# Feed-forward norm in token layout with whole-bank copies, and six row buffers for the first expert blocks

## The chip, the cores and the metric

The kernel runs on one core of one Trainium2 chip. A core has TensorE (PE; its weight loads are listed as PEld), VectorE (DVE), ScalarE (ACT), GpSimd (POOL) and SyncE (SP), which issues most of the transfers between HBM and the on-chip memory SBUF. PE writes its results to PSUM, eight banks of 128 partitions by 512 fp32 words, and DVE and ACT read them there. Each engine works through its own queue in order. The metric is the device time of one execution in microseconds (us); lower is better.

## The reference, cut to what matters

One decoder layer over 512 tokens of 1024 features. Two mixers (a gated recurrence and sparse attention) are projected back and added to the residual stream; then comes an RMS norm with the gain `ffn_norm`, and a mixer of 16384 experts (128 x 128 product keys) that is fed by the normed tokens:

```python
h = h + mixed @ w_out[i]
h = h + peer_ffn(rmsnorm(h, ffn_norm[i]), peer_wq[i], peer_keys[i], peer_u[i], peer_v[i])

def rmsnorm(x, g):
    y = x * rsqrt(mean(x * x, axis=-1, keepdims=True) + EPS)
    return y * g
# peer_ffn, for a block of tokens xt:
q = xt @ wq                                    # 16 groups of 128 columns
s = einsum('thcd,hckd->thck', q, sub_keys)     # scores, then top-16, then experts and weights w
act = gelu(einsum('thkd,td->thk', u[expert], xt))
out = einsum('thk,thkd->td', w * act, v[expert])
```

## The kernel before

The program is written once in Python; a scheduler with priorities sets the order of the instructions on each engine, and memory pools set which buffer a transfer has to wait for. Precise products are made of three passes (`mm3`) over a high and a low half of each operand, and `split` makes the halves: ACT copies the source into the high half, DVE subtracts that from the source into the low half.

The parts that matter here, in order of time:

- **Attention and output projection** (to about 349 us). `out_tile(hf, tt)` transposes one 128-token tile of a mixer's output (4 PE transposes), splits it (`moh`, `mol`), multiplies it by the output weights (24 matmuls for two halves of 512 columns), adds it to the residual `h1` (DVE, L540) and sums squares (ACT, `junk`, L543). The last tile, token tile 0 of the attention half, is left for after the attention: `POST` says ("n",3), ("o",0), ("n",2), ("n",1), ("n",0), where "o" is that `out_tile` and "n" is `ffn_norm`.
- **The feed-forward norm** (`ffn_norm`, once per token tile). POOL makes the reciprocal root `rx`; DVE scales an identity with it (`dg`, L550); eight 128x128 matmuls with `dg` transpose and scale `h1` into two banks (L555); then eight times ACT copies 128 columns, scaled by the gain, into the high half `xTh` (L560; the trace calls the tile aTh), and DVE makes the low half `xTl` (L561; aTl).
- **Query projection and scores** (about 372 to 484 us): 16 rounds `hc`, each with a load of `wq` (tile `wr`), its split, 24 matmuls over `xTh`, `xTl`, and scores with the keys. The keys come in four loads `kr_`, whose halves `kyh`, `kyl` are made in rounds 0, 4, 8 and 12 of the program, that is, where the scheduler puts them.
- **Full blocks** (about 484 to 637 us). The expert table `uT` has 128 blocks of 512 KB. The first 20 are multiplied in full fp32 from the row buffer `ur` directly (L834, 8 matmuls each over `xf`, which the trace shows as two records per matmul), between the matmuls that spread the routing weights (L1036, L1037) into `wd`. `ur` has two buffers. Later blocks are split into `uh`, `ul` first.
- **Main loop** (about 700 to 1640 us): the other blocks, the `v` table, and gathered rows for token tile 0.

Of the kernel before, what the change touches and what calls it, by code (L numbers as in the profile page):

```python
# [10 lines left out]
F32 = mybir.dt.float32  # L11
# [6 lines left out]
ALU = mybir.AluOpType  # L18
# [51 lines left out]
HPLAN = [("h", 0), ("h", 1), ("kv", 0), ("h", 2), ("h", 3)]  # L70
KPLAN = [("q", 0), ("k", 0), ("k", 1), ("s", 0), ("s", 1), ("s", 2), ("s", 3), ("c", 0)]
PLAN = [("b",0),("b",1),("c",),("a",3,(1,2,0),4),("p",),("a",3,(1,2,0),8),("a",3,(1,2,0),ALL),("l",0),("o",0,2),("o",0,0),("o",0,1),("a",2,(1,2,0),5),("a",2,(1,2,0),ALL),("o",0,3),("l",1),("a",1,(1,0,2),ALL),("o",1,3),("o",1,2),("a",0,(1,0,2),3),("a",0,(1,0,2),ALL),("o",1,1)]
POST = [("n",3),("o",0),("n",2),("n",1),("n",0)]
APRI = 150
XB = 6
NP = 3
# [83 lines left out]
def _body(ctx, tc, a, out, dbg=None):  # L160
# [33 lines left out]
    def flat(ap):  # L194
        return ap.rearrange("p a b -> p (a b)")
# [319 lines left out]
            w.append((wh, wl))  # L515
        return w

    def out_tile(pool, pp, tag, bufs, w, hf, tt):
        src = (hv, nq)[hf]
        o = pp.tile([128, 512], F32, name=tag, bufs=bufs)  # L520
        for k in range(4):
            PE.transpose(o[:, k * 128:(k + 1) * 128], src[:, tt, k * 128:(k + 1) * 128], ident)
        mh = pool.tile([128, 4, 128], F32R, name="moh", bufs=MB)
        ml = pool.tile([128, 4, 128], F32R, name="mol", bufs=MB)
        split(flat(mh), flat(ml), o)
        outer = not hf and tt == LAST0
        os_ = [pp.tile([128, 512], F32, name=tag, bufs=bufs) for _ in range(2)] if outer else []
        for k in range(4 if outer else 0):
            for n in range(2):
                ns = slice(n * 512, (n + 1) * 512)  # L530
                mm3(os_[n], mh[:, k], ml[:, k], w[k][0][:, ns], w[k][1][:, ns], k == 0, k == 3)
        for n in range(2):
            ns = slice(n * 512, (n + 1) * 512)
            if outer:
                o = os_[n]
            else:
                o = pp.tile([128, 512], F32, name=tag, bufs=bufs)
                for k in range(4):
                    mm3(o, mh[:, k], ml[:, k], w[k][0][:, ns], w[k][1][:, ns], k == 0, k == 3)
            V.tensor_tensor(h1[:, tt, ns], h1[:, tt, ns], o, op=ALU.add)  # L540
            if hf:
                junk = pool.tile([128, 512], F32, name="junk")
                act(junk, h1[:, tt, ns], AF.Square, accum_out=ss[:, tt, n:n + 1])  # L543

    def ffn_norm(pool, pp, tag, bufs, tt):
        ts = slice(tt * 128, (tt + 1) * 128)
        G.tensor_tensor(rx[:, tt:tt + 1], ss[:, tt, 0:1], ss[:, tt, 1:2], op=ALU.add)
        rstd(rx[:, tt:tt + 1], rx[:, tt:tt + 1], 1, 1.0 / D)
        dg = pool.tile([128, 128], F32, name="dg", bufs=DGB)
        V.tensor_scalar(dg, ident, rx[:, tt:tt + 1], None, op0=ALU.mult)  # L550
        for q in range(2):
            o = pp.tile([128, 512], F32, name=tag, bufs=bufs)
            for k in range(4):
                c = 4 * q + k
                PE.matmul(o[:, k * 128:(k + 1) * 128], lhsT=h1[:, tt, c * 128:(c + 1) * 128], rhs=dg, start=True, stop=True)  # L555
            for k in range(4):
                c = 4 * q + k
                gc = gn[:, G_FFN + c:G_FFN + c + 1]
                ok = o[:, k * 128:(k + 1) * 128]
                act(xTh[:, c, ts], ok, AF.Copy, scale=gc)  # L560
                V.scalar_tensor_tensor(xTl[:, c, ts], ok, gc, xTh[:, c, ts].bitcast(F32), op0=ALU.mult, op1=ALU.subtract)  # L561

    dram = ctx.enter_context(tc.tile_pool(name="dram", bufs=1, space=DRAM))
    ppd = dram.tile([T, D], F32, name="ppd")
# [1 line left out]
    with ExitStack() as e2:  # L566
# [181 lines left out]
        for step in PLAN:  # L748
            if step[0] == "a":
                tt, order, n = step[1:]  # L750
                g = gens.setdefault(tt, attend(tt, order))
                tc.cur_priority -= APRI
                for _ in range(n):
                    next(g, None)
                tc.cur_priority += APRI
            elif step[0] == "b":
                blocks(step[1])
            elif step[0] == "c":
                compress()
            elif step[0] == "p":  # L760
                ple(wop)
            elif step[0] == "l":
                wo_ = out_load(wop, step[1])
            elif step[0] == "n":
                ffn_norm(wop, nps, "tp", NB_TP, step[1])
            else:
                out_tile(wop, nps, "tp", NB_TP, wo_, step[1], step[2])
# [23 lines left out]
    wp = wpx.enter_context(tc.tile_pool(name="wp", bufs=2, reuse_waits="tile"))  # L791
    with ExitStack() as e2:
        ps = e2.enter_context(tc.tile_pool(name="ps2", bufs=6, space=PSUM, reuse_waits="tile"))
        for name, tt in POST:
            if name == "n":
                ffn_norm(wop, ps, "mm", 6, tt)
            else:
                out_tile(wop, ps, "mm", 6, wo_, 1, tt)
        put("h1", h1)
        wox.close()  # L800
        den = ExitStack()
        dense = den.enter_context(tc.tile_pool(name="dense", bufs=2, side="right", reuse_waits="tile"))
        pre = ExitStack()
        prep = pre.enter_context(tc.tile_pool(name="prep", bufs=AHEAD, side="right", reuse_waits="tile"))
# [14 lines left out]
    def a_steps(full):  # L819
        b = nextb[0]  # L820
        nextb[0] += 1
        dq = nc.gpsimd if NPRE - HOLD <= b < NPRE else nc.sync
        ur = dense.tile([128, NC, 128], F32, name="ur")
        dq.dma_start(out=ur, in_=a["uT"][b])
        g_ = prep.tile([128, TD], F32, name="gp") if b < AHEAD else dense.tile([128, TD], F32, name="ga", bufs=3)
        ahead.append(g_ if b < AHEAD or b >= NPRE else None)
# [91 lines left out]
    with ExitStack() as e2:  # L918
# [4 lines left out]
        with ExitStack() as e3:  # L923
# [3 lines left out]
            for hc in range(17):  # L927
# [3 lines left out]
                if hc < 16:  # L931
                    raw = wp.tile([128, NC, 128], F32, name="wr")
                    nc.sync.dma_start(out=raw, in_=a["wq"][:, hc])
                    wh = wp.tile([128, NC, 128], F32R, name="wh")
                    if hc == 0:
                        kyh = wp.tile([128, 16, 128], F32R, name="kyh", bufs=1)
                        kyl = wp.tile([128, 16, 128], F32R, name="kyl", bufs=1)
                    wl = wp.tile([128, NC, 128], F32R, name="wl")
                    split(flat(wh), flat(wl), flat(raw))
                    if hc % 4 == 0:  # L940
                        kr_ = wp.tile([128, 4, 128], F32, name="kr_")
                        nc.sync.dma_start(out=kr_, in_=a["keys"][:, hc:hc + 4])
                        split(kyh[:, hc:hc + 4], kyl[:, hc:hc + 4], kr_)
                    o = ps.tile([128, 512], F32, name="mm")
                    for c in range(NC):
                        mm3(o, wh[:, c], wl[:, c], xTh[:, c], xTl[:, c], c == 0, c == NC - 1)
                    qh = wp.tile([128, T], F32R, name="qh")
                    ql = wp.tile([128, T], F32R, name="ql")
                    split(qh, ql, o)
                    qs.append((qh, ql))  # L950
# [338 lines left out]
```

## Time and profile before

| | us |
|---|---|
| median of 3 runs | 1702.3 (1701.36 to 1702.61) |
| profiled execution, its own time | 1700.27 |
| span of that execution in the trace | 1698.5 |
| mean granted clock of TensorE | 0.993 |

The runs are executions of the same program without a profiler. The profiled execution took 1700.27 us, 1.8 us more than the span from the first to the last instruction. All rows further down are from it, with times counted from the start of the span.

### The profile page before, as it was taken

The numbers are of one execution on the slowest core, as the hardware profiler recorded it, in microseconds if no ns is written. First come the engines' busy times: TensorE is split into PE (matmuls) and PEld (weight loads), VectorE is DVE, ScalarE is ACT, GpSimd is POOL, SyncE is SP. The second block draws the span as 40 slices with busy tenths as digits, with TensorE's granted clock in tenths as the row PEclk, the third lists the DMA queues.
The fourth block names the chain that finished last, engine by engine and source line by source line (L and its number), as shares of the span: only waits on it lengthen the run. The fifth ranks groups of instructions, "written<-read, shape, count | busy, mean of one in ns | idle before, by whom it ended". The sixth has DMA issues, their size and how long they took to land.

```text
span 1698.5 us, 24123 instructions
## 1 busy us (share of the span) xinstructions
PE 1650.0 (97%) x8864; PEld 1416.2 (83%) x8864; DVE 1260.3 (74%) x2485; ACT 745.3 (44%) x1291; POOL 486.1 (29%) x356
## 2 busy tenths in 40 slices
PE   9999999979999999999999999999999999999998
PEld 7887888768866668878899999999999999888987
DVE  6565745659999987865487877777878877787864
ACT  7443664652237875533333333333333333433342
POOL 0013000020000000000055655655545544455610
PEclk9999999989999999999999999999999999999999
DMA  7311130032214689967589898898898988899941
GB/s 256 112 50 49 45 100 25 26 101 86 63 50 146 203 259 287 309 222 239 171 302 327 309 337 313 323 331 325 318 324 323 322 318 322 319 329 333 328 140 50
DMA packets 148647, 373.38 MB, mean 220 GB/s; under 512 B 11990, under 2 KB 59734, under 8 KB 148526
## 3 DMA queue, kind: packets, MB, share of 16 engines
q1 hardware_dynamic: 109808, 231.46, 40.4%
q0 software_dynamic: 38720, 140.38, 23.3%
q8 instruction: 69, 1.13, 0.3%
q14 instruction: 50, 0.41, 0.1%
HBM read 339.02 MB, written 32.77 MB: 219 GB/s over the span
## 4 chain that ended last, share of the span: by engine, by line
PE 50%; issue 17%; DMA 15%; POOL 9%; DVE 5%; ACT 3%; SPq 0%; POOLq 0%; DVEq 0%; ACTq 0%
POOL row L1093 8%; DMA row<-v,eid 7%; PE ac L188 5%; PE ac L186 5%; PE ac L187 5%; PE mm L186 4%; PE mm L187 4%; PE mm L188 4%; PE apsum L834 3%; DMA ur<-uT 3%; DMA row<-u,eid 3%; PE apsum L188 3%; PE apsum L186 3%; PE apsum L187 3%; PE ob L708 2%
## 5 line engine op out<-in xcount | busy, mean ns | idle before, releaser
L188 PE MATMUL ac<-vh,pl 128*128 128x512 f32 x768 | 301.9, 394 | 1.9 <-DVE pl L192 1.7
L1093 POOL DMA_INDIRECT row<-u,eid x128 | 216.2, 1689 | 304.3 <-DVE hn L1097 246.3
L187 PE MATMUL ac<-vl,ph 128*128 128x512 f32 x768 | 301.1, 392 | 0.5 <-DVE vl L192 0.5
L186 PE MATMUL ac<-vh,ph 128*128 128x512 f32 x768 | 299.4, 391 | 1.9 <-ACT vh L191 1.0
L188 PE MATMUL apsum<-aTh,ul 128*128 128x384 f32 x864 | 290.4, 336 | 3.9 <-DVE ul L192 3.9
L186 PE MATMUL apsum<-aTh,uh 128*128 128x384 f32 x864 | 291.5, 337 | 0.5 <-ACT uh L191 0.5
L187 PE MATMUL apsum<-aTl,uh 128*128 128x384 f32 x864 | 289.6, 335 | 0.0
L1093 POOL DMA_INDIRECT row<-v,eid x128 | 208.8, 1631 | 184.0 <-DVE hn L1105 160.4
L191 ACT ACTIVATE uh<-ur 128x1024 fp32r<-128x1024 f32 x108 | 114.5, 1060 | 248.5 <-PE apsum L187 230.1
L192 DVE TENSOR_TENSOR ul<-ur,uh 128x1024 fp32r<-128x1024 f32 x108 | 132.1, 1223 | 78.5 <-ACT uh L191 78.3
L1105 DVE SCALAR_TENSOR_TENSOR hn<-row,cw__7013,hn 128x1024 f32<-128x1024 f32 x128 | 158.6, 1281 | 21.9 <-DMA row<-v,eid 21.7
L188 PEld LDWEIGHTS ac<-vh,pl 128*128 128x128 f32 x768 | 144.1, 188 | 34.8 <-DVE pl L192 4.8
L191 ACT ACTIVATE ph<-ga 128x384 fp32r<-128x384 f32 x118 | 62.0, 525 | 249.3 <-DVE ga L1154 194.6
L186 PEld LDWEIGHTS ac<-vh,ph 128*128 128x128 f32 x768 | 144.4, 188 | 30.7 <-ACT ph L191 2.2
L187 PEld LDWEIGHTS ac<-vl,ph 128*128 128x128 f32 x768 | 144.3, 188 | 29.2 <-DVE vl L192 1.2
L192 DVE TENSOR_TENSOR vl<-vr,vh 128x1024 fp32r<-128x1024 f32 x128 | 156.0, 1219 | 16.0 <-ACT vh L191 16.0
L188 PEld LDWEIGHTS apsum<-aTh,ul 128*128 128x128 f32 x864 | 162.8, 188 | 5.2 <-DVE ul L192 5.2
L191 ACT ACTIVATE vh<-vr 128x1024 fp32r<-128x1024 f32 x128 | 135.2, 1056 | 71.3 <-PE ac L188 70.4
L186 PEld LDWEIGHTS apsum<-aTh,uh 128*128 128x128 f32 x864 | 162.8, 188 | 4.5 <-ACT uh L191 0.6
L187 PEld LDWEIGHTS apsum<-aTl,uh 128*128 128x128 f32 x864 | 162.8, 188 | 3.9
L1097 DVE SCALAR_TENSOR_TENSOR hn<-row,hn 128x1024 f32<-128x1024 f32 x128 | 156.2, 1221 | 3.3 <-DMA row<-u,eid 1.8
L834 PE MATMUL apsum<-xf,ur 128*128 128x384 f32 x320 | 114.7, 503 | 9.5 <-DMA ur<-uT 9.5
(403 smaller groups left out, 2902.7 us busy)
## 6 DMA issues: line engine op xcount, KB each, us to landing
vr<-v SPq DMA_DIRECT2D x128, 512.0 KB, 5.4
ur<-uT SPq DMA_DIRECT2D x125, 512.0 KB, 6.4
xf<-wd SPq DMA_DIRECT2D x30, 768.0 KB, 8.3
wraw<-wi SPq DMA_DIRECT2D x20, 512.0 KB, 4.8
wd<-hn SPq DMA_DIRECT2D x5, 1664.0 KB, 8.7
wd<-stage SPq DMA_DIRECT2D x5, 1664.0 KB, 9.3
wr<-wq SPq DMA_DIRECT2D x16, 512.0 KB, 3.6
wor<-wo SPq DMA_DIRECT2D x16, 256.0 KB, 2.7
```

The source lines that it names most:

```text
L186: PE.matmul(o, lhsT=lh, rhs=rh, start=first, stop=False)
L187: PE.matmul(o, lhsT=lh, rhs=rl, start=False, stop=False)
L188: return PE.matmul(o, lhsT=ll, rhs=rh, start=False, stop=last)
L191: act(hi, src, AF.Copy)
L192: return V.tensor_tensor(lo, src, hi.bitcast(F32), op=ALU.subtract)
L708: PE.matmul(o_ps[:, h], lhsT=pt[:, k * 128:(k + 1) * 128], rhs=kv[:, k, 256 + i * 64:256 + (i + 1) * 64], start=(k == 0), stop=(k == tt))
L834: PE.matmul(o[:, :TD], lhsT=ur[:, c], rhs=xf[:, c], start=c == 0, stop=c == NC - 1)
L1093: G.indirect_dma_start(out=gt, out_offset=None, in_=table, in_offset=bass.IndirectOffsetOnAxis(ap=eid[:, slot:slot + 1], axis=0))
L1097: V.scalar_tensor_tensor(junk, gt, 1.0, xn0, op0=ALU.mult, op1=ALU.mult, accum_out=dots[:, s_:s_ + 1])
L1105: V.scalar_tensor_tensor(ak, gt, cw_[:, s_:s_ + 1], ak, op0=ALU.mult, op1=ALU.add)
```

## The change

Five edits. (1) `ffn_norm` multiplies `h1` by `rx` and by the gain in token layout (DVE, new L562, 512 columns at a time, into `xn`), transposes it plainly with the constant identity, and makes the halves of a whole bank with one `split`, so one ACT copy and one DVE subtraction per bank of four 128x128 blocks. (2) The gain comes as a row, copied to all partitions by one GpSimd transfer (`fg`); `fg` and `xn` lie in `hv`, whose content has been used by then. (3) `out_tile` is cut in two: its transposes and split (`out_turn`, step "t") stand at the head of `POST`. (4) The key splits are held until after the last subtraction of the norm (`issue_after`). (5) For full blocks the row buffers take the names `ur`, `uh`, `ul` in turn, with two buffers each: six. `WLP` is 99, so that the branch for `wl` is never taken; `DGG` is not used.

```diff
-POST = [("n",3),("o",0),("n",2),("n",1),("n",0)]
+KYP = 16
+WLP = 99
+POST = [("t",0),("n",3),("o",0),("n",2),("n",1),("n",0)]
...
-    def out_tile(pool, pp, tag, bufs, w, hf, tt):
+    def out_turn(pool, pp, tag, bufs, hf, tt):
...
         split(flat(mh), flat(ml), o)
+        return mh, ml
+
+    def out_tile(pool, pp, tag, bufs, w, hf, tt, turned=None):
+        mh, ml = turned or out_turn(pool, pp, tag, bufs, hf, tt)
...
+    normed = [None]
+    hvf = hv.rearrange("p t x -> p (t x)")
+    fg, xn = hvf[:, :D], hvf[:, D:]
...
-        dg = pool.tile([128, 128], F32, name="dg", bufs=DGB)
-        V.tensor_scalar(dg, ident, rx[:, tt:tt + 1], None, op0=ALU.mult)
         for q in range(2):
+            qs = slice(q * 512, (q + 1) * 512)
+            V.scalar_tensor_tensor(xn[:, qs], h1[:, tt, qs], rx[:, tt:tt + 1], fg[:, qs], op0=ALU.mult, op1=ALU.mult)
             o = pp.tile([128, 512], F32, name=tag, bufs=bufs)
             for k in range(4):
                 c = 4 * q + k
-                PE.matmul(o[:, k * 128:(k + 1) * 128], lhsT=h1[:, tt, c * 128:(c + 1) * 128], rhs=dg, start=True, stop=True)
-            for k in range(4):
-                c = 4 * q + k
-                gc = gn[:, G_FFN + c:G_FFN + c + 1]
-                ok = o[:, k * 128:(k + 1) * 128]
-                act(xTh[:, c, ts], ok, AF.Copy, scale=gc)
-                V.scalar_tensor_tensor(xTl[:, c, ts], ok, gc, xTh[:, c, ts].bitcast(F32), op0=ALU.mult, op1=ALU.subtract)
+                PE.transpose(o[:, k * 128:(k + 1) * 128], xn[:, c * 128:(c + 1) * 128], ident)
+            xh, xl = (x[:, 4 * q:4 * q + 4, ts] for x in (xTh, xTl))
+            normed[0] = split(xh, xl, o.rearrange("p (k t) -> p k t", t=128))
...
             elif step[0] == "l":
+                if step[1]:
+                    nc.gpsimd.dma_start(out=fg, in_=a["fgain"].to_broadcast([128, D]))
                 wo_ = out_load(wop, step[1])
...
-        ur = dense.tile([128, NC, 128], F32, name="ur")
+        ur = dense.tile([128, NC, 128], F32, name=("ur", "uh", "ul")[b % 3] if full else "ur")
...
                         kr_ = wp.tile([128, 4, 128], F32, name="kr_")
                         nc.sync.dma_start(out=kr_, in_=a["keys"][:, hc:hc + 4])
-                        split(kyh[:, hc:hc + 4], kyl[:, hc:hc + 4], kr_)
+                        if hc < KYP:
+                            with tc.issue_after(normed[0].ins):
+                                split(kyh[:, hc:hc + 4], kyl[:, hc:hc + 4], kr_)
```

How the queues change. First ACT, from the end of the attention: `moh` is the high half of the last output tile, `aTh` that of the norm, `wh` that of a `wq` load, `kyh` that of a key load. Before:

```order
L543 ACTIVATE junk,ss<-h_63 128x512 x2
L560 ACTIVATE aTh<-mm,gn 128x128 x3
L191 ACTIVATE wh<-wr 128x1024
L560 ACTIVATE aTh<-mm,gn 128x128 x2
L191 ACTIVATE moh<-mm 128x512
```

Now, at the same place of ACT's queue:

```order
L550 ACTIVATE junk,ss<-h_63 128x512 x2
L194 ACTIVATE moh<-mm 128x512
L194 ACTIVATE aTh<-mm 128x4x128 x2
L194 ACTIVATE wh<-wr 128x1024
L194 ACTIVATE kyh<-kr__3540 128x512
```

`moh` had five norm copies and one weight copy ahead of it and now has none.

Second DVE, from the last addition of the output tile (L540 before, L547 now) to the first split of round 2: `h` is `h1`, `kyl` the low half of the keys, `hn` in the new rows is `xn`. Before:

```order
L192 TENSOR_TENSOR kyl<-kr__3850,kyh 128x512
L192 TENSOR_TENSOR kyl<-kr__4142,kyh 128x512
L540 TENSOR_TENSOR h_63<-h_63,mm 128x512
L561 SCALAR_TENSOR_TENSOR aTl<-mm,gn,aTh 128x128
L550 TENSOR_SCALAR dg<-cst,rx 128x128
L561 SCALAR_TENSOR_TENSOR aTl<-mm,gn,aTh 128x128 x2
L192 TENSOR_TENSOR kyl<-kr__4434,kyh 128x512
L561 SCALAR_TENSOR_TENSOR aTl<-mm,gn,aTh 128x128 x10
L550 TENSOR_SCALAR dg<-cst,rx 128x128
L561 SCALAR_TENSOR_TENSOR aTl<-mm,gn,aTh 128x128 x11
```

Now:

```order
L547 TENSOR_TENSOR h_63<-h_63,mm 128x512
L562 SCALAR_TENSOR_TENSOR hn<-h_63,rx,hn 128x512
L195 TENSOR_TENSOR aTl<-mm,aTh 128x4x128 x3
L562 SCALAR_TENSOR_TENSOR hn<-h_63,rx,hn 128x512 x3
L195 TENSOR_TENSOR aTl<-mm,aTh 128x4x128 x3
L195 TENSOR_TENSOR kyl<-kr__3540,kyh 128x512
L195 TENSOR_TENSOR kyl<-kr__3803,kyh 128x512
L195 TENSOR_TENSOR kyl<-kr__4095,kyh 128x512
L195 TENSOR_TENSOR kyl<-kr__4387,kyh 128x512
L195 TENSOR_TENSOR wl<-wr,wh 128x1024
```

Between the last addition and the scaling of tile 0 (the last `dg` before, the last two L562 now) stood thirteen subtractions, a `dg` and a key split; now there are three subtractions and the two L562 of tile 1. All four key splits stand behind the norm.

Third SP's loads, from the second key load on (`kr_` keys, `wr` query weights, `ur`, `uh`, `ul` row buffers of the full blocks). Before:

```order
L942 DMA kr__4142<-keys 128x512
L933 DMA wr<-wq 128x1024
L942 DMA kr__4434<-keys 128x512
L824 DMA ur<-uT 128x1024 x2
L933 DMA wr<-wq 128x1024 x12
L824 DMA ur<-uT 128x1024 x7
```

Now:

```order
L945 DMA wr<-wq 128x1024 x2
L836 DMA ur<-uT 128x1024
L836 DMA uh<-uT 128x1024
L836 DMA ul<-uT 128x1024
L836 DMA ur<-uT 128x1024
L958 DMA kr__4095<-keys 128x512
L958 DMA kr__4387<-keys 128x512
L836 DMA uh<-uT 128x1024
L836 DMA ul<-uT 128x1024
L945 DMA wr<-wq 128x1024 x12
```

Six blocks of `uT` instead of two are loaded before the twelve query weights, and the last two key loads stand behind four of them.

## Rows read from the trace of the kernel before

**Rows 1.** The page's head.

```profile
span 1698.5 us, 24123 instructions
```

**Rows 2.** Stretches: length, busy PE, PEld, DVE, ACT, POOL (instructions), granted clock, DMA share, GB/s.

```profile
346.00:372.00 26.00, 18.00 (x98) 15.70 (x96) 16.09 (x40) 14.64 (x39) 9.15 (x13) 0.84 0.32 102
372.00:484.00 112.00, 112.00 (x578) 94.31 (x577) 100.24 (x492) 26.10 (x37) 2.04 (x3) 0.99 0.20 57
484.00:560.00 76.00, 70.25 (x372) 44.75 (x372) 75.63 (x305) 50.48 (x105) 0.00 (x0) 0.98 0.41 125
560.00:640.00 80.00, 72.97 (x508) 49.53 (x507) 65.65 (x132) 60.16 (x135) 0.00 (x0) 0.98 0.82 242
640.00:700.00 60.00, 55.63 (x457) 52.29 (x454) 45.87 (x64) 30.75 (x40) 5.92 (x7) 0.97 0.94 293
800.00:1600.00 800.00, 799.11 (x4025) 723.57 (x4024) 623.61 (x767) 292.32 (x389) 406.74 (x245) 1.00 0.87 313
```

**Rows 3.** Chain of waits, 346 to 376 us: start, us, what.

```profile
349.07 2.91 PE mm L555 x16
...
359.95 4.18 DMA kr__4434<-keys
...
365.50 2.29 DVE aTl L561 x9
...
368.03 0.37 DVE dg L550
368.44 3.78 PE mm L555 x16
372.23 0.43 PE mm L186
...
374.94 0.23 PE mm L188
```

**Rows 4.** Timeline, 346 to 372 us: start, us, engine, line, operation, idle before.

```profile
349.65 0.19 ACT L543 ACTIVATION_READ_ACCUMULATOR junk<-h 128x1 f32 x1
...
353.71 0.60 ACT L191 ACTIVATE moh<-mm 128x512 fp32r<-128x512 f32 x1
...
360.42 0.40 PE L188 MATMUL mm<-woh,mol 128*128 128x512 f32 x1
...
363.14 0.55 POOL L181 TENSOR_TENSOR rx<-rx,mhalf 128x1 f32<-128x1 f32 x1
```

**Rows 5.** Groups by line, 346 to 376 us: count, busy us, mean ns, idle before.

```profile
L560 ACT ACTIVATE aTh<-mm,gn 128x128 fp32r<-128x128 f32 x32 | 10.3, 365 | 5.3 <-PE mm L555 2.8 <-DVE aTl L561 2.3
L561 DVE SCALAR_TENSOR_TENSOR aTl<-mm,gn,aTh 128x128 fp32r<-128x128 f32 x32 | 9.7, 345 | 5.6 <-ACT aTh L560 5.6
...
L192 DVE TENSOR_TENSOR kyl<-kr__4434,kyh 128x512 fp32r<-128x512 f32 x1 | 0.7, 691 | 1.4 <-ACT kyh L191 1.4
```

**Rows 6.** Single lines, whole trace: min/median/max ns, first and last start.

```profile
L522 PEld LDWEIGHTS tp<-cst,hn x28: 138/141/198, 236.1 to 339.5; 128*128 128x128 f32 x28
L522 PEld LDWEIGHTS mm<-cst,hn x4: 230/230/231, 351.5 to 352.2; 128*128 128x128 f32 x4
L232 DVE SCALAR_TENSOR_TENSOR aTl<-hn,gn,aTh x8: 746/752/754, 6.1 to 16.7; 128x512 fp32r<-128x512 f32 x8
```

**Rows 7.** Waits of PE and SP, 512 to 640 us: us, times, longest.

```profile
PE apsum L834 <- DMA ur<-uT: 9.5, 5, 2.4
SPq L824 <- PE apsum L834: 42.6, 9, 10.1
```

**Rows 8.** Waits of PE, 560 to 640 us.

```profile
PE apsum L834 <- DMA ur<-uT: 7.0, 4, 2.2
```

**Rows 9.** Chain of waits, 340 to 700 us: its longest piece of loading.

```profile
535.78 10.45 DMA ur<-uT
```

**Rows 10.** Timeline of DVE, 318 to 348 us: the first dg, in the attention's tail.

```profile
330.88 0.28 DVE L550 TENSOR_SCALAR dg<-cst,rx 128x128 f32<-128x128 f32 x1 [1.41 <-POOL rx L181]
```

**Rows 11.** Transfers issued from 330 to 400 us: KB each, us to landing.

```profile
kr__4434<-keys SPq DMA_DIRECT2D x1, 256.0 KB, 4.2
ur<-uT SPq DMA_DIRECT2D x2, 512.0 KB, 5.0
```

More of the change, by code (lines that the diff above doesn't have):

```diff
@@ L72 @@
 PLAN = [("b",0),("b",1),("c",),("a",3,(1,2,0),4),("p",),("a",3,(1,2,0),8),("a",3,(1,2,0),ALL),("l",0),("o",0,2),("o",0,0),("o",0,1),("a",2,(1,2,0),5),("a",2,(1,2,0),ALL),("o",0,3),("l",1),("a",1,(1,0,2),ALL),("o",1,3),("o",1,2),("a",0,(1,0,2),3),("a",0,(1,0,2),ALL),("o",1,1)]
-POST = [("n",3),("o",0),("n",2),("n",1),("n",0)]
+DGG = 1
+KYP = 16
+WLP = 99
+POST = [("t",0),("n",3),("o",0),("n",2),("n",1),("n",0)]
 APRI = 150
@@ L793, in _body @@
         ps = e2.enter_context(tc.tile_pool(name="ps2", bufs=6, space=PSUM, reuse_waits="tile"))
+        turned = None
         for name, tt in POST:
@@ L796, in _body @@
                 ffn_norm(wop, ps, "mm", 6, tt)
+            elif name == "t":
+                turned = out_turn(wop, ps, "mm", 6, 1, tt)
             else:
-                out_tile(wop, ps, "mm", 6, wo_, 1, tt)
+                out_tile(wop, ps, "mm", 6, wo_, 1, tt, turned)
         put("h1", h1)
@@ L938, in _body @@
                     wl = wp.tile([128, NC, 128], F32R, name="wl")
-                    split(flat(wh), flat(wl), flat(raw))
+                    if hc == WLP:
+                        with tc.issue_after(normed[0].ins):
+                            split(flat(wh), flat(wl), flat(raw))
+                    else:
+                        split(flat(wh), flat(wl), flat(raw))
                     if hc % 4 == 0:
@@ L942, in _body @@
                         nc.sync.dma_start(out=kr_, in_=a["keys"][:, hc:hc + 4])
-                        split(kyh[:, hc:hc + 4], kyl[:, hc:hc + 4], kr_)
+                        if hc < KYP:
+                            with tc.issue_after(normed[0].ins):
+                                split(kyh[:, hc:hc + 4], kyl[:, hc:hc + 4], kr_)
+                        else:
+                            split(kyh[:, hc:hc + 4], kyl[:, hc:hc + 4], kr_)
                     o = ps.tile([128, 512], F32, name="mm")
```

## The prediction, made blind

> **What bounds the kernel now.** I read the stage table first [rows 2]. From 800 to 1600 us TensorE is busy for 799.11 of 800 us at its full clock, so in the long second half nothing but PE's own work counts, and time saved earlier is kept to the end. The stretch of the query projection, 372 to 484, is as full: 112.00 of 112. Two earlier stretches have holes in PE. In 346 to 372, the hand-over from attention to the expert mixer, PE is busy for 18.00 of 26 us and its granted clock averages 0.84, a mix of 2.4 and 1.2 GHz. In 560 to 640 it is busy for 72.97 of 80. The change touches both.
>
> The chain of waits through the first hole [rows 3] shows a queue. PE gets the first norm products at 349.07; the last output tile's matmuls cannot start until ACT has made `moh`, at 353.71 + 0.60 = 354.31, and end at 360.42 + 0.40 [rows 4]. Then the chain goes through a key load (4.18 us from 359.95), a key split and nine subtractions `aTl` on DVE to the last `dg` at 368.03, PE's last eight products (3.78 us) and the first projection matmul at about 372.2. But `rx` for that `dg` was ready at 363.14 + 0.55 = 363.69 [rows 4]: the scaling stood 4.3 us in DVE's queue behind work of other tiles, one piece of which waited for a load (the key split: 1.4 us idle before it [rows 5]). ACT and DVE also take turns in the norm: 5.3 and 5.6 us idle before their 32 small operations [rows 5].
>
> In the second hole every wait of PE is for a row buffer: 9.5 us in five waits from 512 to 640, 7.0 of them after 560 [rows 7, 8]. SP's loads in turn wait 42.6 us for PE to release one of two buffers [rows 7], and one load then takes up to 10.45 us to land [rows 9].
>
> **The norm, step by step.** The work hardly shrinks on DVE: 32 operations of 345 ns and four `dg` become eight scalings and eight subtractions of 512 columns. A 512-column operation of the same kind on SBUF takes 752 ns, a subtraction of that width 691 [rows 5, 6]; I take 0.7 for both. ACT gets eight copies of about 0.6 us (`moh` has that shape [rows 4]) for 32 of 365 ns. PE's transposes load in 138 to 141 ns each, 230 when its clock is low [rows 6]. What changes is the order.
>
> 1. PE starts at 349.07 as before: it still waits for the additions of the attention's end. Four transposes for `moh` and eight of tile 3 take 12 x 0.14 = 1.7 us, or 12 x 0.23 = 2.8 at 1.2 GHz. In 349.07 to 352 PE showed 2.91 us for 16 records, partly slow, so I take 2.2: to 351.3.
> 2. ACT is free at 349.65 + 0.19 = 349.84, now with nothing ahead of `moh`: done at 350.45, 3.9 us earlier than 354.31. The matmuls start at 351.3, 3.0 earlier than before. They took 354.37 to 360.82, 6.45 us, including products I now count elsewhere; but they now lie in the stretch of low clock and some run at 0.43 us apart, as at 372.23, instead of 0.23, as at 374.94 [rows 3]. I take 7.0: end at 358.3, a gain of 2.5.
> 3. From there to `rx` of tile 0 took 363.69 - 360.82 = 2.9 us before: addition, squares, POOL. The same now: `rx` at 361.2.
> 4. DVE's queue between is two scalings and three subtractions, 5 x 0.6 to 0.7 = 3 to 3.5 us from the last addition's end at about 359, so the scaling of tile 0 starts at about 362.2: 1.0 late instead of 4.3. Then 0.7 for the scaling, 4 x 0.23 = 0.9 for the transposes, 0.6 for the copy: 364.4, and the first projection matmul starts on the high half, while DVE makes the low half that the second one needs. Say 364.5, against 372.2. Gain 7.7.
> 5. Given back: the first matmuls of the projection run at half clock now too, and perhaps longer, as the dozen transposes ahead of them leave PE mostly idle: 0.6. And two scalings of tile 3 replace its `dg` in the attention's tail: at 330.88 a 0.28 us operation becomes 0.7, ahead of a softmax row maximum, the second one lies in a gap [rows 10]: 0.6.
>
> **Sum for the norm: 7.7 - 1.2 = 6.5 us.** Bounds: all of steps 1 and 2 at low clock (matmuls 10.3 instead of 7.0) gives 3.2; none of it, and no loss in the tail, gives 9.5.
>
> **The key splits** move 4 x 0.69 us of DVE work to behind the norm. Their cover is the projection, where DVE is busy for 100.24 of 112 [rows 2]; its next work there, the split of round 2, waits for PE's first round anyway, some 6 us. But `kyl` of the third and fourth loads now waits for transfers that SP issues only when the first two splits are done, at about 366. A key load landed in 4.2 us, and a 512 KB row buffer in 5.0 beside it [rows 11]. With 4.2 the last key split ends at 371.5 and the split of round 2 at 373 or so, while PE needs it two rounds after its start, at 364.5 + 2 x 5.6 = 375.7 (24 matmuls of 0.23 a round). Price zero, 2.7 us to spare; if the cover is gone it costs what the load is late beyond that. The gain row's transfer is one GpSimd issue, which waits for the transposes of the recurrent half's last tile to be through with `hv`; queued behind it are small POOL operations of the attention tiles that follow. Its first reader is the scaling at 330.88 [rows 10], a whole attention tile later in the program. I count zero; at worst one landing like the 5.0 us of rows 11, which would be a small mishap inside the range.
>
> **Six row buffers.** All six blocks are loaded during 357 to 484, when the transfer engines are busy for 0.20 to 0.32 of the time [rows 2], and SP stays four loads ahead afterwards. This takes 4 x 0.5 = 2.1 MB out of the crowded stretch after 512, some 7 us of the 293 GB/s that 640 to 700 moves. Each of PE's five waits was a load that was issued when the buffer came free two blocks earlier; with four more blocks of lead, about 4 x 5 us of full-block matmuls, all should go: at most 9.5. But the first, 2.4 us, lies where DVE is busy for 75.63 of 76: there DVE is the limit and a waiting PE costs nothing [rows 2]. After 560 DVE has 65.65 of 80 and ACT 60.16, so 73 us of PE work without waits would leave them 7 us of room. **I take 7.0 - 0 = 7.0**; bounds 2.5 (ACT and DVE, dense in part of the stretch, take most of it) and 9.5.
>
> After 640 the blocks use two buffers again and nothing is added. I count zero, plus or minus 2.
>
> **Sum:** 6.5 + 7.0 = 13.5. The profiled execution took 1700.27 us for its span of 1698.5 [rows 1], so it would go to 1686.8. The median of the runs is 2.0 above that execution, 1702.3, so the forecast is **1688.8 us**, 0.8% faster. A measurement of this kernel tells about 0.2%, 3.4 us, from no change.
>
> **Rivals.**
>
> *The row buffers give little* (chance 0.22). PE stops waiting for loads, and waits for the operands that DVE and ACT make in the same stretch. For: 75.63 of 76 on DVE before 560. Against: in 560 to 640 both have over 14 us idle. Gain 2.5 instead of 7: 1693.3.
>
> *The last key loads come late* (0.10). Four row buffers are issued before them. The Trainium skill, in DMA: Bandwidth & Descriptors, section Queues, rings and completion order, says that on each DMA engine descriptors are taken in ring order; by that rule a key load waits for whatever of the four row buffers is still unread. The trace has a load that took 10.45 us behind others [rows 9]. If the last key load takes that long it lands at 376.5, DVE's split of round 2 ends at about 379.4, and PE stands for 3.7 us: 1692.5. Rows 11, with two row buffers in flight and 4.2 us, speak against it.
>
> *Given back* (0.05). The gathers for tile 0, not PE, set the end. Then both gains become idle time and the result is 1702. Against: 799.11 of 800.
>
> *Slower* (0.03). The same late key loads, but long enough to lose everything: DVE stands still in its queue behind `kyl`, and the whole projection with it. Before, DVE's split of round 2 ended about 9 us after PE's first projection matmul, near 381. For a result of 1706 it would have to end some 13.5 + 3.7 us later than it now needs to, at about 393, so the last key load would have to take over 24 us. The slowest in these rows is 10.45.
>
> The forecast's own case has 0.60. Its range is 1682 to 1692; with the first two rivals, 1682 to 1697 holds about 0.85, and I keep that. Faster by over 0.2%: 0.60 + 0.22 + 0.10 = 0.92; within 0.2%: 0.05; slower: 0.03.
>
> **What would show it.** In the profile after: `moh` of the last output tile at about 350 us; the first `wq` matmul at about 364.5; no DVE wait for a key load longer than 4 us, and no hole in PE near 375; PE's waits for `uT` between the norm and 640 near zero; the first two-buffer block at about 623 instead of 637; PE full in the second half and the end about 13 us earlier. Wrong if PE's low clock covers the whole output tile, if DVE waits for ACT in the new norm as it did in the old, or if the waits for loads come back as waits for DVE and ACT.

## The result, and the profile after

Four runs of each kernel on one chip: 1684.86 us with the change, 1701.83 before, a ratio of 0.990 with a 95% interval of 0.9883 to 0.9917. A second timing beside the experiments gave 1681.82 against 1700.5, ratio 0.9893 [0.9876, 0.9911]. So the change takes 17.0 and 18.7 us off. The forecast was 1688.8, a gain of 13.5: the direction and the stages were right, the size was 3.5 to 5 us too small.

The page's head of the changed kernel; the execution took 1686.05 us.

```profile
span 1684.3 us, 24014 instructions
```

Stretches of the changed kernel, with the columns of [rows 2]:

```profile
346.00:372.00 26.00, 20.08 (x84) 15.77 (x83) 19.32 (x25) 11.11 (x22) 12.87 (x16) 0.80 0.39 139
372.00:484.00 112.00, 112.00 (x577) 93.52 (x576) 103.34 (x513) 25.26 (x33) 0.81 (x1) 1.00 0.23 69
484.00:560.00 76.00, 70.81 (x387) 45.11 (x386) 75.43 (x284) 53.73 (x115) 0.00 (x0) 0.98 0.46 136
560.00:640.00 80.00, 80.00 (x610) 58.97 (x609) 74.93 (x139) 65.03 (x136) 0.00 (x0) 1.00 0.87 260
800.00:1600.00 800.00, 799.06 (x4037) 724.94 (x4036) 629.27 (x770) 293.03 (x390) 420.46 (x251) 1.00 0.88 315
```

Against [rows 2]: from 560 to 640 TensorE has no hole left (80.00 of 80, before 72.97), the second half is as full as it was, and the hand-over still has one, at a low average clock again (0.80, before 0.84).

The hand-over in the timeline of the changed kernel (start, us, engine, line, operation), from the attention's last addition to the first projection matmul:

```profile
349.70 0.68 DVE L547 TENSOR_TENSOR h<-h,tp 128x512 f32<-128x512 f32 x1
351.13 0.60 ACT L194 ACTIVATE moh<-mm 128x512 fp32r<-128x512 f32 x1
358.91 0.39 PE L191 MATMUL mm<-woh,mol 128*128 128x512 f32 x1
361.88 0.55 POOL L184 TENSOR_TENSOR rx<-rx,mhalf 128x1 f32<-128x1 f32 x1
362.67 0.74 DVE L562 SCALAR_TENSOR_TENSOR hn<-h,rx,hn 128x512 f32<-128x512 f32 x1
362.84 9.97 POOL L942 TENSOR_TENSOR xf<-aTh,aTl 128x384 f32<-128x384 f32 x8 [0.41 <-DVE aTl L195]
363.33 1.48 DVE L562 SCALAR_TENSOR_TENSOR hn<-h,rx,hn 128x512 f32<-128x512 f32 x1
364.74 1.48 DVE L562 SCALAR_TENSOR_TENSOR hn<-h,rx,hn 128x512 f32<-128x512 f32 x1
367.04 0.78 PE L189 MATMUL mm<-aTh,wh 128*128 128x512 f32 x1
```

The order is the one forecast: `moh` comes early, the scaling of tile 0 follows its `rx` closely. But the two scalings of tile 0 take 1.48 us each, where the one ahead of them, which began before GpSimd's additions, took 0.74; they run just while GpSimd makes `xf`.

The waits of TensorE and of SP's queue from 512 to 640 in the changed kernel (us, times, longest), which answer to [rows 7]:

```profile
PE wm L1006 <- DVE f32i L1003: 0.8, 1, 0.8
PE wm L1005 <- DVE f32i L1002: 0.8, 1, 0.8
...
SPq L836 <- PE apsum L846: 40.2, 9, 10.7
```

No wait for a row buffer is left. SP still waits for TensorE nearly as long as before (42.6 us), but with the longer lead TensorE does not wait for its loads.

**How the executions are compared.** Two profiled executions are not a pair that can simply be subtracted. The sixth row maximum of 512 columns on VectorE, in the attention, stands at a different time in each, long before the stretches that the change touches. Timelines of VectorE: the kernel before and the changed one (three maxima merged in one line), and `xf_behind` (below; the first of the three alone):

```profile
201.06 1.89 DVE L699 TENSOR_REDUCE nm<-sc 128x1 f32<-128x512 f32 x3
201.79 1.89 DVE L706 TENSOR_REDUCE nm<-sc 128x1 f32<-128x512 f32 x3
205.82 0.69 DVE L706 TENSOR_REDUCE nm<-sc 128x1 f32<-128x512 f32 x1
```

So I cut every execution at the same events into six stretches: A from that row maximum to the start of the attention's last addition `h` (349.70 above); B from there to the first projection matmul; C to the last score matmul; D to the end of the last full block; E to the first matmul `ac` of the dense part; F to the end. The times are differences of timeline rows, in us:

| kernel | A | B | C | D | E | F |
|---|---|---|---|---|---|---|
| before | 147.28 | 23.54 | 112.02 | 153.07 | 65.39 | 996.14 |
| changed | 147.91 | 17.34 | 113.13 | 143.21 | 64.57 | 996.35 |
| changed, second profile | 148.22 | 17.34 | 111.71 | 142.98 | 64.46 | 993.32 |
| `six_only` | 147.51 | 22.08 | 111.31 | 143.98 | 64.04 | 995.48 |
| `norm_only` | 147.85 | 17.37 | 111.71 | 148.68 | 67.79 | 996.65 |
| `no_key_hold` | 148.00 | 17.99 | 112.63 | 143.25 | 63.83 | 998.38 |
| `no_turn` | 147.88 | 19.58 | 112.23 | 142.97 | 64.70 | 998.60 |
| `four` | 147.96 | 17.35 | 111.60 | 144.14 | 64.56 | 995.81 |
| `xf_late` | 148.13 | 16.09 | 112.12 | 142.97 | 64.15 | 997.39 |
| `xf_behind` | 147.88 | 15.82 | 112.75 | 142.88 | 65.24 | 995.61 |
| `filled` | 147.84 | 17.34 | 111.59 | 142.98 | 64.46 | 994.07 |

The gain stands in B (6.2 us) and D (9.9), and 0.8 in E. B repeats to 0.03 us in four executions that share the norm's order (17.34, 17.34, 17.37, 17.35), so it tells more than a run's time does. With the old norm it repeats less well: 23.54 us in the kernel before and 22.08 in `six_only`. TensorE's last eight norm products, which the trace shows as sixteen records, took 3.78 us in the one [rows 3], at a granted clock of 0.50, and 2.05 in the other, at 1.00:

```profile
370.18 2.05 PE L555 MATMUL mm<-dg,h 128*128 128x128 f32 x16 [3.04 <-DVE dg L550]
```

So the 6.2 holds against the kernel before as profiled; against `six_only` it is 4.7.

C and F scatter by 1.8 and 5 us. C's scatter has one place: from the first to the 25th projection matmul (one round) the eleven executions take between 5.93 and 7.73 us, and from there to the end of C all eleven take 105.39. The granted clock is at 1.2 GHz for a longer or shorter part of this round in all but `six_only` and `filled`. For F I found no order that the edits would explain.

### The profile page after: what moved, and what is told of

It is laid out like the page before. It is cut to its first block, busy times and chain, and to the rows that moved or that the text cites. A ratio compares the mean times of both kernels' runs of the same rounds, so it can differ in the third digit from the quotient of the medians.

```text
span 1684.3 us, 24014 instructions
## 1 busy us (share of the span) xinstructions
PE 1644.0 (98%) x8832; PEld 1410.5 (84%) x8832; DVE 1262.6 (75%) x2465; ACT 739.1 (44%) x1267; POOL 491.1 (29%) x357
## 4 chain that ended last, share of the span: by engine, by line
PE 64%; issue 12%; DMA 10%; DVE 7%; POOL 5%; ACT 2%; POOLq 0%; DVEq 0%; SPq 0%; ACTq 0%
DMA row<-v,eid 8%; PE ac L191 7%; PE ac L190 7%; PE ac L189 7%; PE apsum L189 5%; PE apsum L191 5%; PE apsum L190 5%; PE mm L189 4%; PE mm L191 4%; PE mm L190 4%; POOL row L1113 4%; PE apsum L846 3%; PE ob L715 2%; PE pt L712 1%; PE tp L191 1%
## 5 line engine op out<-in xcount | busy, mean ns | idle before, releaser
L1113 POOL DMA_INDIRECT row<-v,eid x128 | 212.8, 1662 | 179.4 <-DVE hn L1125 153.3
L195 DVE TENSOR_TENSOR pl<-ga,ph 128x384 fp32r<-128x384 f32 x118 | 65.9, 558 | 71.7 <-ACT ph L194 71.7
```

The source lines that it names most:

```text
L195: return V.tensor_tensor(lo, src, hi.bitcast(F32), op=ALU.subtract)
L1113: G.indirect_dma_start(out=gt, out_offset=None, in_=table, in_offset=bass.IndirectOffsetOnAxis(ap=eid[:, slot:slot + 1], axis=0))
```

## The experiments

Eight more kernels, and the changed kernel once more, each timed in five rounds beside the kernel before.

**The row buffers alone** (`six_only`), in the kernel before:

```diff
-        ur = dense.tile([128, NC, 128], F32, name="ur")
+        ur = dense.tile([128, NC, 128], F32, name=("ur", "uh", "ul")[b % 3] if full else "ur")
```

> The kernel before with the six row buffers alone; norm, key splits and order of the last output tile as before. In the two traces the stretch from the last score matmul to the last full-block matmul went from 153.1 us (483.90 to 636.97) to 143.1 (480.28 to 623.38). Theory A, the buffers alone do this: no wait of TensorE for a row buffer between 512 and 640 (9.5 us before), the stretch at 143 us, the run about 9.9 us faster than before, 1692. Rival B, VectorE limits the part before 560 as the prediction had it: 2.5 to 7.0 us, 1695 to 1699, and the waits come back as waits for VectorE. Rival C, part of the shorter stretch came from the norm being earlier: less than 7 us here, and more than 4 in the run with the norm alone.

Measured: 1689.85 us against 1701.49, ratio 0.9935 [0.9917, 0.9953], a gain of 11.6 by the medians. D is 143.98. The waits of TensorE from 512 to 640:

```profile
PE wm L986 <- DVE f32i L983: 0.8, 1, 0.8
PE wm L985 <- DVE f32i L982: 0.8, 1, 0.8
```

Theory A: all waits for loads gone with the old norm too, and D is 9.1 shorter. The interval is 8.0 to 14.1 us, so not only the forecast's lower bound of 2.5 is out but its 7.0 as well.

**The norm alone** (`norm_only`), the changed kernel with two row buffers:

```diff
-        ur = dense.tile([128, NC, 128], F32, name=("ur", "uh", "ul")[b % 3] if full else "ur")
+        ur = dense.tile([128, NC, 128], F32, name="ur")
```

> The changed kernel with two row buffers, so the norm, the key splits and the early output tile alone. Theory A: the norm is worth what the traces show at the end of the projection, 3.7 us, or 4.7 if the 0.9 us by which the profiled execution of the changed kernel was already late at 207 us belongs to that execution and not to the change: 1697 to 1698. TensorE waits 9.5 us for row buffers again. Rival B, the forecast's own term: 6.5 us, 1695.3. Rival C, the two parts help each other: less than 3 us alone.

Measured: 1693.27 us, ratio 0.9945 [0.9925, 0.9965], a gain of 8.2. The waits from 512 to 640, first row:

```profile
PE apsum L846 <- DMA ur<-uT: 6.8, 4, 2.3
```

The gain is above every theory's: A's 3.7 to 4.7 lie below the interval (which begins at 0.35%, 6 us), B's 6.5 at its low end. The profile says why A was too low: C, which cost the first profiled execution 1.1 us, costs nothing here (111.71), and the 9.5 us of waits came back as 6.8, so D is 4.4 shorter than before; 2.4 of that is lost again in E (67.79). What the two buffers cost is best read from D and E together: 216.47 here against 207.78 and 207.44 with six buffers, 8.7 to 9.0 us; with the old norm 218.46 against 208.02, 10.4. The parts sum to 19.8 alone and gave 17.0 and 18.7 together; with intervals of some 3 us on each, an overlap is not shown.

**GpSimd's additions behind the norm** (`xf_late`, `xf_behind`). The additions get a one-column copy ahead of them that reads the norm's last low half:

```diff
                 if hc == 4:
-                    for c in range(NC):
+                    gt = wp.tile([128, 1], F32, name="gt", bufs=1)
+                    gate = G.tensor_copy(gt, xTl[:, NC - 1, 0:1].bitcast(F32))
+                    with tc.issue_after(gate.ins):
+                      for c in range(NC):
```

In `xf_late` the copy went to `rx[:, 0:1]`, which the kernel reads again after the mixer: there the later use of tile 0's norm factor is changed, the work is not.

> The changed kernel with GpSimd's eight additions that make xf held behind a one-column copy on GpSimd that reads the last low half of the norm; nothing else moved. In the changed kernel the two scalings of tile 0 took 1.48 us each beside these additions, and 0.75 elsewhere. Theory A, VectorE and GpSimd are in each other's way when both read SBUF: the scalings of tile 0 take 0.75, and from the start of the first of them to the first projection matmul it is about 2.3 us instead of 3.71 (363.33 to 367.04), so the run is about 1.4 us faster, 1683.4, which the runs' times can hardly tell; the additions then slow key splits or the split of the second round, which has 1 us to spare. Rival B, the scalings are slow for another reason (transfers that land, the clock): they stay at 1.48. The Trainium skill, SBUF — State Buffer, section Who interferes with whom, has a VectorE instruction with two SBUF inputs contend with a GpSimd instruction that reads SBUF; by that rule it is theory A.

> As xf_late, the changed kernel with GpSimd's eight additions behind a one-column copy of the last low half, but the copy goes to a column of its own, so that the whole reference is computed. Theory A as there: tile 0's scalings 0.75 us each, 2.2 to 2.4 us from the first of them to the first projection matmul instead of 3.71, key splits beside the additions about 1.5 instead of 0.69, the run about 1.4 us faster than the changed kernel and 17 to 18 faster than before. Rival B, the key splits, now slowed, hold up the split of the second round by more than 1 us, and TensorE has a hole near 377: no faster than the changed kernel.

The single lines of `hn`, `xf` (min/median/max ns) and `kyl` (one duration each) in the changed kernel:

```profile
L562 DVE SCALAR_TENSOR_TENSOR hn<-h,rx,hn x8: 740/750/1483, 331.8 to 364.7; 128x512 f32<-128x512 f32 x8
L942 POOL TENSOR_TENSOR xf<-aTh,aTl x8: 1004/1437/1462, 362.8 to 371.8; 128x384 f32<-128x384 f32 x8
L195 DVE TENSOR_TENSOR kyl<-kr__3540,kyh x1: 897/897/897, 368.7 to 368.7; 128x512 fp32r<-128x512 f32 x1
L195 DVE TENSOR_TENSOR kyl<-kr__3803,kyh x1: 1493/1493/1493, 369.5 to 369.5; 128x512 fp32r<-128x512 f32 x1
L195 DVE TENSOR_TENSOR kyl<-kr__4095,kyh x1: 692/692/692, 373.2 to 373.2; 128x512 fp32r<-128x512 f32 x1
L195 DVE TENSOR_TENSOR kyl<-kr__4387,kyh x1: 693/693/693, 375.4 to 375.4; 128x512 fp32r<-128x512 f32 x1
```

The same lines in `xf_behind`:

```profile
L562 DVE SCALAR_TENSOR_TENSOR hn<-h,rx,hn x8: 741/744/753, 335.8 to 368.2; 128x512 f32<-128x512 f32 x8
L945 POOL TENSOR_TENSOR xf<-aTh,aTl x8: 1001/1230/1997, 371.8 to 380.0; 128x384 f32<-128x384 f32 x8
L195 DVE TENSOR_TENSOR kyl<-kr__3540,kyh x1: 681/681/681, 371.1 to 371.1; 128x512 fp32r<-128x512 f32 x1
L195 DVE TENSOR_TENSOR kyl<-kr__3805,kyh x1: 686/686/686, 371.7 to 371.7; 128x512 fp32r<-128x512 f32 x1
L195 DVE TENSOR_TENSOR kyl<-kr__4097,kyh x1: 1470/1470/1470, 376.3 to 376.3; 128x512 fp32r<-128x512 f32 x1
L195 DVE TENSOR_TENSOR kyl<-kr__4389,kyh x1: 1499/1499/1499, 377.7 to 377.7; 128x512 fp32r<-128x512 f32 x1
```

Theory A, twice over. Read the last column of times against GpSimd's: whichever VectorE operation falls into the additions takes up to twice as long, the last two scalings and the first two key splits in the one kernel, the last two key splits in the other. B falls from 17.34 to 15.82 (`xf_late`: 16.09), so the collision cost 1.25 to 1.5 us. Rival B of `xf_behind`, a hole near 377, is not there: C is 112.75, inside its scatter, and the part of it behind the first round takes the same 105.39 us as everywhere. The times (1683.66 and 1684.99 us, ratios 0.9896 and 0.9907) cannot tell either kernel from the changed one, as expected.

**The key splits not held** (`no_key_hold`):

```diff
-KYP = 16
+KYP = 0
```

> The changed kernel with the low key halves not held behind the norm, so that they stand in VectorE's and the high halves in ScalarE's queue among the norm's operations as before the change. Theory A, the hold is part of the gain: one key split lies ahead of the last scaling of tile 0 and two more ahead of its last subtraction, each 0.7 to 1.5 us: the first projection matmul is 0.7 to 1.5 us later, the thirteenth 2 to 3.5 us, the run 1 to 3.5 us slower than the changed kernel, 1686 to 1688. Rival B, they lie in gaps of VectorE: no change at the first projection matmul. Rival C, the hold makes the third and fourth key load later and costs more than it gives: faster than the changed kernel, with the split of the second round earlier than 376.4.

Measured: 1685.56 us, ratio 0.9908 [0.989, 0.9926]; B is 17.99, 0.65 later than with the hold. That is just under the lower end of theory A at the first matmul, and more than B repeats to, so rival B is out. But the thirteenth matmul, for which theory A had 2 to 3.5 us, is 0.2 and 1.6 us later than in the two profiles of the changed kernel, counted from the attention's last addition: that part did not come. The run's time does not tell the two kernels apart, so rival C's gain is not there either.

**No early turn** (`no_turn`):

```diff
-POST = [("t",0),("n",3),("o",0),("n",2),("n",1),("n",0)]
+POST = [("n",3),("o",0),("n",2),("n",1),("n",0)]
```

> The changed kernel without the early turn of the last output tile: its four transposes and its copy moh stand behind those of tile 3's norm again. In the changed kernel moh ran from 351.13 to 351.73, its output matmuls from 352.39 to 359.30. Theory A, the early turn is part of the gain: on TensorE eight transposes (1.65 us) stand ahead of the four, on ScalarE two copies of 0.55 ahead of moh, so moh is done 1.2 to 1.9 us later, the output matmuls end 0.7 to 1.9 later, the first projection matmul with them, and the run is about 1 us slower than the changed kernel, 1686, which the times alone can hardly tell. Rival B, the turn buys nothing, since matmuls that start later meet TensorE's full clock sooner: output matmuls end within 0.3 us of where they did, counted from the last addition of the attention.

Measured: 1686.06 us, ratio 0.992 [0.9901, 0.994]; B is 19.58, 2.2 later. Its `moh`, 2.81 us after the start of the last addition (348.92) instead of 1.43:

```profile
351.73 0.60 ACT L194 ACTIVATE moh<-mm 128x512 fp32r<-128x512 f32 x1 [0.26 <-PE mm L525]
```

The stretch of the output matmuls, in `no_turn` and then in the changed kernel:

```profile
352.38:360.75 8.37, 8.37 (x29) 6.75 (x30) 4.31 (x5) 3.61 (x6) 0.00 (x0) 0.70 0.41 128
```

```profile
352.39:359.30 6.91, 6.91 (x30) 5.56 (x29) 5.70 (x8) 4.39 (x8) 0.00 (x0) 0.85 0.27 78
```

Theory A, a little over its range, but the 2.2 us are two things. Counted from the last addition the output matmuls begin 0.77 us later, which is the order; they also take 1.46 us longer, at a granted clock of 0.70 instead of 0.85. Whether the missing turn brings the longer spell at 1.2 GHz, one execution cannot say: the old norm had a short spell at this place in the kernel before and a long one in `six_only`. So the turn is worth 0.8 us, and up to 2.2, of B's 6.2.

**Four row buffers** (`four`):

```diff
-name=("ur", "uh", "ul")[b % 3] if full else "ur")
+name=("ur", "uh")[b % 2] if full else "ur")
```

> The changed kernel with four row buffers for the full blocks in place of six. Theory A, it is the lead that counts: a load is issued two blocks earlier than with two buffers, some 9 us of TensorE's work (143 us for 40 blocks and what lies between is 3.6 a block), and the longest wait with two buffers was 2.4 us, so no wait of TensorE for a row buffer is left, and the stretch from the last score matmul to the last full block takes 143 to 144 us as with six. Rival B, it is the early loading of all six blocks that counts, which takes 2.1 MB out of the crowded stretch: with four buffers half of the gain is lost, waits of 3 to 5 us, stretch 147 to 149.

Measured: 1686.36 us, ratio 0.991 [0.9886, 0.9935]; D is 144.14, and no wait for a row buffer is in the trace. Theory A: it is the lead that counts, and two more buffers would have done. The expectation's working is off, though: D holds 20 full blocks, not 40, so a block and what lies beside it is some 7.2 us and two blocks are a lead of some 14, not 9.

**TensorE kept busy before the projection, and the changed kernel once more** (`filled`, `after_again`). The fill, in the norm of tile 0, on top of `xf_behind`:

```diff
+        if tt == 0:
+            fill = pp.tile([128, 512], F32, name=tag, bufs=bufs)
+            for _ in range(10):
+                PE.matmul(fill[:, :384], lhsT=xTh[:, 0, 128:256], rhs=xTh[:, 0, 128:], start=True, stop=True)
```

> The kernel with the additions of xf behind the norm, plus ten matmuls of 384 columns on TensorE between the transposes of tile 1 and those of tile 0, whose result is never read. In the run without them TensorE was idle for most of the 4 us before tile 0's transposes (2.16 us in one piece), and after it the granted clock was 0.50 in the first 2.5 us of the projection, whose matmuls came 0.43 us apart instead of 0.23. Theory A, the low clock is what the idle time leaves behind: with the fill the first round's 24 matmuls take about 5.6 us from the first of them, against 7.0 there, and the run is about 1 us faster than without the fill, which its times can hardly tell; at worst the fill ends 0.5 us after tile 0's scaling. Rival B, the clock falls for another reason: the first round takes 7.0 us again and the fill only delays the transposes.

> The changed kernel once more, beside the fill on one chip. From the line at 207 us of the kernel before (the row maximum of 512 columns at which the profiled executions stand 201.0 to 205.8 us from their start) to the end it takes 1482 to 1483 us in the profile, as in its first profile (1482.5), and the first scaling of tile 0 to the first projection matmul about 3.7 us. By the runs with one part alone (11.6 and 8.2 us) the two parts would give 19.8 if they simply added, and the first timing gave 17.0: a ratio near 0.990 again says that they overlap, one near 0.988 that they add.

`after_again` is the second timing above. Its profile missed what was expected of it: from the row maximum to the end it took 1478.1 us, where the first profile had 1482.5 (1.4 us of that lie in C's first round and 3.0 in F), and its ratio lies between the two that were to tell an overlap from a plain sum. `filled` took 1683.18 us, ratio 0.9896 [0.9879, 0.9913]. The stretch 367 to 372 in the changed kernel's two profiles, then in `filled` (columns as in [rows 2], the granted clock third from the end):

```profile
367.00:372.00 5.00, 5.00 (x15) 3.88 (x14) 3.34 (x4) 0.60 (x1) 5.00 (x6) 0.55 0.18 57
```

```profile
367.00:372.00 5.00, 5.00 (x20) 4.03 (x20) 2.93 (x4) 0.60 (x1) 5.00 (x5) 0.90 0.22 63
```

```profile
367.00:372.00 5.00, 5.00 (x23) 4.00 (x23) 1.84 (x3) 1.08 (x2) 5.00 (x6) 1.00 0.63 206
```

With the fill the clock is at its full level from the first projection matmul on, and from the first to the 25th matmul it takes 6.20 us against 7.36 in `xf_behind`. But the same changed kernel shows 7.73 in one execution and 6.32 in the other, and `four`, which has no fill, shows 6.21, so the one profile with the fill settles nothing: theory A is not shown. And the fill stood in the way: B is 17.34 again, 1.5 more than without it, since its ten matmuls ran from 362.18 to 364.02 while tile 0's transposes waited behind. No gain.

No version beats the changed kernel by an amount that the times can show; `xf_behind` is 1.5 us better in the stretch that it touches.

## Why the prediction was right, and where its sizes were off

**The norm, steps 1 to 4.** Counted from the start of the attention's last addition (348.34 before, 349.70 after), the forecast and the changed kernel are: `moh` done at 2.1 and 2.0; output matmuls ended at 10.0 and 9.6; `rx` of tile 0 at 12.9 and 12.7; scaling of tile 0 begun at 13.9 and 13.6. Every link held to 0.4 us. The one that failed is the last: from that scaling to the first projection matmul step 4 has 2.3 us, 0.7 for the scaling, and it was 3.71. The scaling took 1.48, and the second one behind it too. The step took VectorE's price from rows in which GpSimd stood still. (The first projection matmul before started at 371.88, not 372.2, so the forecast's 7.7 is 7.4 between these events, against 6.2 measured.)

What I overlooked was that the change itself makes the collision. Before, the additions ran from 366.36 beside the old norm's subtractions, which take their operand from PSUM, and neither was slow; the additions of the kernel before (min/median/max ns), and the subtractions on VectorE that ran partly beside them:

```profile
L930 POOL TENSOR_TENSOR xf<-aTh,aTl x8: 992/997/1008, 366.4 to 373.0; 128x384 f32<-128x384 f32 x8
365.42 2.69 DVE L561 SCALAR_TENSOR_TENSOR aTl<-mm,gn,aTh 128x128 fp32r<-128x128 f32 x10
```

The new scalings take `h` and the gain row, both from SBUF, and there the additions slow down too (median 1437 ns above). The subtractions of the new norm, with one operand in PSUM, ran beside them unslowed, 1.27 us for two (a pair took 1.28 at 353.19, with GpSimd idle):

```profile
366.14 1.27 DVE L195 TENSOR_TENSOR aTl<-mm,aTh 128x512 fp32r<-128x512 f32 x2
```

By the Trainium skill, SBUF — State Buffer, section Who interferes with whom, a VectorE instruction with two SBUF inputs contends with a GpSimd instruction that reads SBUF, and one with at most one SBUF input outside the two-port modes does not; these traces agree on both halves. With the price measured here, some 0.7 us more for each of the two scalings, the first projection matmul would have been put at 366 instead of 364.5; the measured B of 17.34 us is 365.7 in the forecast's times.

**Step 5, given back.** The tail term of 0.6 held: A is 147.3 and 147.5 with the old norm, 147.8 to 148.2 with the new. The clock term of 0.6 is not a constant: C was 1.1 longer in one profile of the changed kernel and 0.3 shorter in the other, and all of that lies in the projection's first round.

**The norm's sum.** 6.5 forecast; B less A's tail gives 5.6 (4.1 with the B of `six_only` as the old one), and a run with the norm alone gained 8.2, with an interval that holds 6.5. That interval, some 3 us to either side, cannot show what the stretches do: the collision was missing from the sum.

**The key splits.** Price zero was right, by another path: the third and fourth key load were issued only at 369.59 and 371.04, not at 366, and the last split ended 4.6 us later than I had it. Transfers of the changed kernel (KB, us to landing), then its timeline:

```profile
kr__4095<-keys SPq DMA_DIRECT2D x1, 256.0 KB, 2.9
kr__4387<-keys SPq DMA_DIRECT2D x1, 256.0 KB, 3.7
```

```profile
375.44 0.69 DVE L195 TENSOR_TENSOR kyl<-kr__4387,kyh 128x512 fp32r<-128x512 f32 x1 [1.57 <-ACT kyh L194]
376.40 1.22 DVE L195 TENSOR_TENSOR wl<-wr,wh 128x1024 fp32r<-128x1024 f32 x1 [0.26 <-ACT wh L194]
...
381.66 0.45 PE L189 MATMUL mm<-aTh,wh 128*128 128x512 f32 x1
```

The split of the third weight block ended at 377.62, and TensorE took it up at 381.66: 4 us to spare, where the forecast had 2.7. The rival of late key loads did not happen, and ring order behind the row buffers was not put to the test: the four row buffers ahead of them were issued at 359.34 to 360.71, some 9 us earlier.

**The row buffers.** This is the term that was mis-sized: 7.0 forecast, 9.1 in D with the buffers alone, 9.9 and 10.1 in the changed kernel, 8.7 to 10.4 in D and E together, 11.6 in the time of the buffers alone. The waits themselves went nearly as argued: 9.5 us vanished, and the waits for VectorE's `f32i` in D rose from 3.3 to 4.9 (`six_only`) and 5.2, so 7.9 and 7.6 net; that the first 2.4 would buy little, VectorE being full there, was about right. What was missing stands in TensorE's busy time. D as a whole, in the kernel before, `six_only` and the changed kernel:

```profile
483.90:636.97 153.07, 140.29 (x847) 91.51 (x847) 141.15 (x437) 109.12 (x236) 0.00 (x0) 0.98 0.61 183
483.30:627.28 143.98, 139.00 (x847) 91.32 (x847) 139.43 (x436) 108.25 (x236) 0.00 (x0) 0.98 0.60 180
480.17:623.38 143.21, 138.02 (x847) 90.77 (x847) 139.37 (x436) 108.21 (x236) 0.00 (x0) 0.99 0.61 181
```

With the buffers alone TensorE is busy for 1.3 us less, for the same matmuls at the same granted clock of 0.98. An estimate from the rows of the kernel before accounts for most of it: a full-block matmul takes 0.49 us in its row and the next one starts 0.32 us after it, so ahead of a load wait 0.16 us stay uncovered; behind the wait the second matmul starts 0.40 to 0.43 us after the first (588.81, 605.60 and 631.54), another 0.1. That is some 0.26 us a wait that does not count as waiting, 1.3 for the five, less what two short waits for `f32i` cost in their place.

The changed kernel's D is shorter than that of `six_only` by another 0.8 us, and that goes with the clock: with six or four buffers D takes 142.9 to 143.3 us in the seven executions whose granted clock averages 0.99, and 143.98 and 144.14 in the two with 0.98 (`six_only`, `four`). The kernel before ran a part at 1.2 GHz right behind a load wait (0.86 from 572 to 584), but a load wait is neither needed for that nor enough: `six_only` has no load wait in D and the low average all the same, and `norm_only` waited 6.8 us and kept its clock at 1.00 from 512 to 640.

**After 640.** Zero forecast; E is 0.8 and 0.9 shorter in the two profiles, inside the plus or minus 2.

**What stays open.** The sizing errors have opposite signs, 0.9 too much for the norm and 2.9 too little for the row buffers, so it is partly luck that the sum missed by no more. The measured terms add to 6.2 - 0.6 + 9.9 + 0.8, about 16 us. The rest of the 17.0 to 18.7 lies within what C, F and the old norm's B vary from one execution to the next, and I cannot put it to a cause. Why the spell at 1.2 GHz is longer in one execution than in another of the same kernel is open too.

## What to carry to other kernels

When an edit changes where an operand comes from (PSUM to SBUF here), price the operation beside what the other engines do at that moment, not by its duration in a quiet row; GpSimd's work was free in the old order and stood on the path in the new. When TensorE waits for loads, a lead of two more buffers was enough, and the gain was the waits less what returned as other waits, plus, by the estimate above, a quarter of a microsecond of busy time for each stop. For effects of 1 us in 1700, cut executions at fixed events: a stretch repeated to 0.03 us where the runs' times scatter by several. Read the granted clock in each stretch as well: between two executions of the old norm it made a difference as large as some of the effects sought.

## What the runs showed of the hardware that I had not expected

- VectorE's 128x512 operations with both operands in SBUF took 1.47 to 1.50 us beside GpSimd's additions instead of 0.68 to 0.75, and the additions 1.43 to 1.46 instead of 1.00.
- Executions reach the same instruction in the attention between 200.1 us (`filled`) and 205.8 us (`xf_behind`) after their start, though these two kernels differ only behind it.
- The spell at 1.2 GHz at the start of the projection differs between executions of one kernel: from the first to the 25th matmul 7.73 and 6.32 us. From there to the last score matmul all eleven executions take 105.39 us.
